# Group softmax on one core: the first tile's load and store cut into pieces of 5 and 11 groups, and the last wait put into a section of its own on SyncE

## The chip, the cores and the metric

The kernel runs on one core of a Trainium2 chip. The metric is the device time of one launch in microseconds; the time before is the median of 4 runs. A profile of one further execution shows what each engine and each DMA queue did.

## The reference

```python
def setup_inputs():
    B, N, D, G = 4, 4096, 4352, 8
    return {"x": np.random.randn(B, N, D).astype(np.float32)}

def reference(x):
    B, N, D = x.shape
    G = 8
    Dg = D // G
    x_g = x.reshape(B, N, G, Dg)
    x_g = x_g - x_g.max(axis=-1, keepdims=True)
    exp = np.exp(x_g)
    out = exp / exp.sum(axis=-1, keepdims=True)
    return out.reshape(B, N, D).astype(np.float32)
```

Each of the 16,384 rows of 4352 numbers is cut into 8 groups of 544, and a softmax is taken over each group. The input and the output are 285.2 MB each.

## The kernel before

**Tiles.** A tile holds 256 rows: 128 partitions with 2 rows each, so 8704 numbers (34,816 bytes) or 16 groups in a partition, 4.456 MB in all. There are 64 tiles (`nt`) and six buffers in SBUF (`xt0` to `xt5`, `NT = 6`); tile t lives in buffer t modulo 6 from its load to its store, and is worked on in place.

**One tile's way.** SyncE (SP) issues its load (L126). ScalarE (ACT) takes the exponential of the whole tile in one instruction (L73). VectorE (DVE) sums each group (L83), takes the reciprocals (L85) and multiplies (L88). Then the tile is stored: GpSimd (POOL) issues the stores of tiles 0 to 61 (L138), SP those of the last two tiles, 62 and 63 (L134). No maximum is subtracted on this way. VectorE keeps the largest sums and reciprocals (L96), tests them after the last tile (`judge`, L101 to L119, with a small matmul on PE), and three engines read the verdict into registers (L167); only where a number was out of bounds would all be done again with the maximum (L168 to L202). With this input that does not happen: the branch skips it.

**Order.** The order is written out by hand with semaphores, and each engine's instructions run in the order of the program. `landed[b]` counts loads into buffer b, `stored[b]` GpSimd's stores from it, `exp_done` ACT's tiles, `scaled` VectorE's, `last_stored` the two stores that SP issues; a DMA adds 16 when it has landed. SP issues loads 0 to 5 at once; before each load t from 6 on it waits until the store of tile t - 6 has landed (L123). The last tile, 63, is loaded as two DMAs of one row of each partition (L129), and ACT and VectorE work on it in two halves (`parts`). After the loads SP waits for tile 62, stores it, waits for tile 63 and stores it.

GpSimd waits for `scaled` and issues, tile by tile. After store 61 it waits until stores 58 to 61 have landed (L140), drains (L141), and waits for both of SP's last stores (L142).

**The section.** All of this stands in one critical section (L49), in which nothing is scheduled or synchronised but by the program's own semaphores. Its `sync_engine` is GpSimd: GpSimd opens the section for all engines, and at its end all engines wait until GpSimd has come to the end of its own instructions. Behind the section the program ends with barriers over all engines (L228).

**Queues.** All DMAs run on the core's same 16 DMA engines, each DMA with 8 of its 128 partitions on each of them. What SP issues is in queue 1 (the loads and the last two stores), what GpSimd issues is in queue 0.

Of the kernel before, what the change touches and what calls it, by code (L numbers as in the profile page):

```python
# [9 lines left out]
def kernel(  # L10
# [5 lines left out]
    nc = tc.nc  # L16
    G = 8
    P = 128
    R = 2
    NT = 6  # L20
# [3 lines left out]
    N, D = xf.shape  # L24
    Dg = D // G
    nt = N // (P * R)
    LAST = 2
    TURNS = 6
    LOW, HIGH = 1e-6, 1e30
    f32 = mybir.dt.float32  # L30
    X = mybir.AxisListType.X
# [2 lines left out]
    xt = xf.rearrange("(t p r) d -> t p (r d)", p=P, r=R)  # L34
    ot = of.rearrange("(t p r) d -> t p (r d)", p=P, r=R)

    landed = [tc.alloc_semaphore(f"landed{b}") for b in range(NT)]
    stored = [tc.alloc_semaphore(f"stored{b}") for b in range(NT)]
    last_landed = tc.alloc_semaphore("last_landed")
    last_stored = tc.alloc_semaphore("last_stored")  # L40
    exp_done = tc.alloc_semaphore("exp_done")
    own = tc.alloc_semaphore("own")
    scaled = tc.alloc_semaphore("scaled")
# [2 lines left out]
    judged = tc.alloc_semaphore("judged")  # L46
    again = {k: tc.alloc_semaphore(f"again_{k}") for k in ("in", "max", "exp", "rec", "out", "end")}

    ctx.enter_context(tc.tile_critical(  # L49
        sync_engine=mybir.EngineType.Pool, no_gpsimd_drain=True))  # L50
    bufs = [ctx.enter_context(nc.sbuf_tensor(f"xt{b}", [P, R * D], f32)) for b in range(NT)]
    vals = ctx.enter_context(nc.sbuf_tensor("vals", [P, NT, 2, RG], f32))
# [12 lines left out]
    def grouped(b):  # L65
        return bufs[b][:, :].rearrange("p (g d) -> p g d", d=Dg)

    def groups(t, g):
        return grouped(t % NT)[:, g, :]

    def scalar_exp(n):
        t, g = parts[n]
        i = nc.scalar.activation(out=groups(t, g), in_=groups(t, g), func=Exp, scale=1.0)  # L73
        if g.start == 0:
            i.wait_op(landed[t % NT], 16 * (t // NT + 1), "sem-ge")
        else:
            i.wait_op(last_landed, 16, "sem-ge")
        i.then_inc(exp_done, 1)

    def vector_scale(n, exp_at, at):  # L80
        t, g = parts[n]
        b = t % NT
        nc.vector.reduce_sum(out=vals[:, b, 0, g], in_=groups(t, g), axis=X).wait_op(  # L83
            exp_done, exp_at, "sem-ge").then_inc(own, 1)
        nc.vector.reciprocal(out=vals[:, b, 1, g], in_=vals[:, b, 0, g]).wait_op(  # L85
            own, at + 1, "sem-ge").then_inc(own, 1)
        xg = groups(t, g)
        nc.vector.tensor_tensor(  # L88
            out=xg,
            in0=xg,  # L90
            in1=vals[:, b, 1, g].unsqueeze(2).to_broadcast([P, g.stop - g.start, Dg]),
            op=op.mult,
        ).wait_op(own, at + 2, "sem-ge").then_inc(scaled, 1)
# [7 lines left out]
    def judge(at):  # L101
# [16 lines left out]
        nc.vector.wait_ge(tested, 5)  # L118
        nc.vector.tensor_copy(out=verdict[:, :], in_=count[:, :]).then_inc(judged, 1)  # L119

    for t in range(nt):
        if t >= NT:
            nc.sync.wait_ge(stored[t % NT], 16 * (t // NT))  # L123
        tile_in = bufs[t % NT]
        if t < nt - 1:
            nc.sync.dma_start(out=tile_in[:, :], in_=xt[t]).then_inc(landed[t % NT], 16)  # L126
        else:
            for r in range(R):
                nc.sync.dma_start(  # L129
                    out=tile_in[:, r * D:(r + 1) * D], in_=xt[t, :, r * D:(r + 1) * D],  # L130
                ).then_inc(landed[t % NT] if r < R - 1 else last_landed, 16)
# [1 line left out]
        nc.sync.wait_ge(scaled, t + 1 if t < nt - 1 else len(parts))  # L133
        nc.sync.dma_start(out=ot[t], in_=bufs[t % NT][:, :]).then_inc(last_stored, 16)  # L134

    for t in range(nt - LAST):
        nc.gpsimd.wait_ge(scaled, t + 1)
        nc.gpsimd.dma_start(out=ot[t], in_=bufs[t % NT][:, :]).then_inc(stored[t % NT], 16)  # L138
    for t in range(nt - NT, nt - LAST):
        nc.gpsimd.wait_ge(stored[t % NT], 16 * (t // NT + 1))  # L140
    nc.gpsimd.drain()  # L141
    nc.gpsimd.wait_ge(last_stored, 16 * LAST)  # L142

    nc.scalar.preload_act_table(Exp)  # L144
    for n in range(len(parts)):
        scalar_exp(n)

    nc.vector.memset(peak[:, :, :, :], 0.0).then_inc(own, 1)  # L148
    with nc.vector.Fori(0, TURNS):  # L149
        for n in range(NT):  # L150
# [4 lines left out]
    done = 1  # L155
    for n in range(TURNS * NT, len(parts)):
        vector_scale(n, n + 1 - TURNS * NT, done)
        done += 2
# [9 lines left out]
    with nc.If_cmp(regs, 2 * P, "IS_LT"):  # L168
# [3 lines left out]
        with nc.Fori(0, nt, engines=[ET.SP, ET.Activation, ET.DVE]) as t:  # L172
# [11 lines left out]
            for g in range(RG):  # L184
                i = nc.scalar.activation(
                    out=grouped(0)[:, g, :], in_=grouped(0)[:, g, :], func=Exp,
# [6 lines left out]
                out=mx[:, :], in_=grouped(0), axis=X, negate=True).then_inc(again["max"], 1)  # L193
# [6 lines left out]
                out=grouped(0), in0=grouped(0),  # L200
                in1=vals[:, 0, 1, :].unsqueeze(2).to_broadcast([P, RG, Dg]),
                op=op.mult).then_inc(again["out"], 1)  # L202


# [1 line left out]
_INS = ['x']  # L206
# [26 lines left out]
```

## Time and profile before

The median of 4 runs is 1324.55 us (1324.49 to 1325.65). The profiled execution took 1324.64 us; its span, from the first to the last instruction, is 1322.9 us, so 1.7 us lie outside the span.

| | us | of the span |
|---|---|---|
| VectorE busy (213 instructions) | 1199.7 | 91% |
| ScalarE busy (66) | 478.7 | 36% |
| GpSimd busy (66) | 33.3 | 3% |
| TensorE busy (2) | 0.2 | 0% |

Each engine's busy share in 40 equal slices of the span, in tenths, and what the DMA engines moved in each slice:

```profile
DVE  3999999999998998989989889898898988989894
ACT  4443342432424424234243342433424334243231
DMA  9999999999999999999999999999999999999999
GB/s 404 421 436 424 437 438 434 425 438 436 432 430 438 436 425 436 438 434 425 438 436 432 430 438 436 425 437 437 434 426 437 436 433 430 437 435 426 437 437 389
```

The two queues' shares of the 16 engines' span add up to 99.9%, and 570.47 MB were moved at a mean of 431 GB/s:

```profile
DMA packets 18580, 570.47 MB, mean 431 GB/s; under 512 B 2064, under 2 KB 2064, under 8 KB 2064
...
q1 hardware_dynamic: 9648, 294.13, 51.6%
q0 software_dynamic: 8928, 276.30, 48.3%
```

The costliest groups of instructions (times called, then busy us and the mean ns of one, then idle us of the engine before them and what ended it):

```profile
L73 ACT ACTIVATE xt<-xt 128x8704 f32<-128x8704 f32 (+1 forms) x65 | 477.4, 7345 | 814.7 <-DMA xt<-in_x_dram 814.7
L83 DVE TENSOR_REDUCE vals<-xt 128x16 f32<-128x8704 f32 (+1 forms) x65 | 590.1, 9078 | 100.9 <-ACT xt L73 100.0
L88 DVE TENSOR_TENSOR xt<-xt,vals 128x8704 f32<-128x8704 f32 (+1 forms) x65 | 590.5, 9085 | 2.2
L138 POOL DMA_DIRECT2D out_dram<-xt x62 | 33.1, 534 | 1232.6 <-DVE xt L88 1232.6
```

The times from issue to landing hold the waiting in the queue: 40.9 us for a load and 55.9 us for one of GpSimd's stores (medians). In the waits of SP's queue, 57 waits of a load for the store of its buffer make up 1195.5 us.

### The profile page before, as it was taken

What the parts mean: (1) busy time and instruction counts of PE and PEld (TensorE: products, weight loads), DVE (VectorE), ACT (ScalarE), POOL (GpSimd) and SP (SyncE); (2) the same over time, 40 slices, a digit from 0 to 9 for tenths busy, and PEclk for the clock granted to TensorE, in tenths of its full rate; (3) what the DMA queues carried; (4) which work ended last, traced back from release to release, by engine and by line L of the source; (5) the groups of instructions that cost most, each with busy time, mean ns of one, the idle gap of its engine ahead of it and who ended that gap; (6) DMA issues with size and microseconds to landing.
All of it is one profiled execution on the core that took longest, in us unless ns stands there. A gap on an engine that the chain in (4) does not pass through costs nothing.

```text
span 1322.9 us, 513 instructions
## 1 busy us (share of the span) xinstructions
PE 0.2 (0%) x2; PEld 0.1 (0%) x2; DVE 1199.7 (91%) x213; ACT 478.7 (36%) x66; POOL 33.3 (3%) x66
## 2 busy tenths in 40 slices
PE   0000000000000000000000000000000000000000
PEld 0000000000000000000000000000000000000000
DVE  3999999999998998989989889898898988989894
ACT  4443342432424424234243342433424334243231
POOL 0000000000000000000000000000000000000000
DMA  9999999999999999999999999999999999999999
GB/s 404 421 436 424 437 438 434 425 438 436 432 430 438 436 425 436 438 434 425 438 436 432 430 438 436 425 437 437 434 426 437 436 433 430 437 435 426 437 437 389
DMA packets 18580, 570.47 MB, mean 431 GB/s; under 512 B 2064, under 2 KB 2064, under 8 KB 2064
## 3 DMA queue, kind: packets, MB, share of 16 engines
q1 hardware_dynamic: 9648, 294.13, 51.6%
q0 software_dynamic: 8928, 276.30, 48.3%
q14 instruction: 4, 0.03, 0.0%
HBM read 285.21 MB, written 285.21 MB: 431 GB/s over the span
## 4 chain that ended last, share of the span: by engine, by line
another core or an unknown queue 66%; DMA 7%; DVE 6%; SPq 1%; ACT 1%; issue 0%; PE 0%; DVEq 0%
DMA out_dram<-xt 4%; DMA xt<-in_x_dram 3%; DVE xt L88 3%; DVE vals L83 3%; SPq L126 1%; ACT xt L73 1%; DVE vals L85 0%; DVE extreme L103 0%; DVE peak L96 0%; DVE within L109 0%; PE found L113 0%; DVE count L117 0%; DVE verdict L119 0%; DVEq L149 0%
## 5 line engine op out<-in xcount | busy, mean ns | idle before, releaser
L73 ACT ACTIVATE xt<-xt 128x8704 f32<-128x8704 f32 (+1 forms) x65 | 477.4, 7345 | 814.7 <-DMA xt<-in_x_dram 814.7
L83 DVE TENSOR_REDUCE vals<-xt 128x16 f32<-128x8704 f32 (+1 forms) x65 | 590.1, 9078 | 100.9 <-ACT xt L73 100.0
L88 DVE TENSOR_TENSOR xt<-xt,vals 128x8704 f32<-128x8704 f32 (+1 forms) x65 | 590.5, 9085 | 2.2
L138 POOL DMA_DIRECT2D out_dram<-xt x62 | 33.1, 534 | 1232.6 <-DVE xt L88 1232.6
L85 DVE RECIPROCAL vals<-vals 128x16 f32<-128x16 f32 (+1 forms) x65 | 16.3, 251 | 2.2
L96 DVE TENSOR_TENSOR peak<-peak,vals 128x192 f32<-128x192 f32 x11 | 3.9, 352 | 0.0
L144 ACT ACT_TABLE_LOAD x1 | 1.3, 1283 | 0.9 <-PEq L217 0.9
L148 DVE MEMSET peak<- 128x192 f32 x1 | 0.2, 218 | 1.1 <-PEq L217 1.1
L117 DVE TENSOR_REDUCE count<-found 1x1 f32<-1x2 f32 x1 | 0.1, 147 | 0.3 <-PE found L113 0.3
L103 DVE TENSOR_REDUCE extreme<-peak 128x2 f32<-128x192 f32 x1 | 0.3, 348 | 0.0
L113 PE MATMUL found<-within,one 128*1 128x2 f32 x2 | 0.2, 166 | 1306.0 <-DVE within L109 1306.0
L109 DVE TENSOR_SCALAR within<-extreme 128x1 f32<-128x1 f32 x2 | 0.2, 148 | 0.0
L119 DVE CAST verdict<-count 1x1 int32<-1x1 f32 x1 | 0.1, 143 | 0.0
L113 PEld LDWEIGHTS found<-within,one 128*1 128x1 f32 x2 | 0.1, 82 | 1306.0 <-DVE within L109 1306.0
L217 POOL MEMSET const-float32-0.0<- 128x1 f32 x1 | 0.1, 98 | 0.3 <-issue 0.3
L217 POOL MEMSET const-bfloat16-1.0<- 128x1 bf16 x1 | 0.1, 101 | 0.0
L217 POOL MEMSET const-uint8-127<- 128x1 uint8 x1 | 0.1, 99 | 0.0
L217 POOL MEMSET const-float32-1.0<- 128x1 f32 x1 | 0.1, 98 | 0.0
L102 DVE MEMSET one<- 128x1 f32 x1 | 0.1, 59 | 0.0
## 6 DMA issues: line engine op xcount, KB each, us to landing
xt<-in_x_dram SPq DMA_DIRECT2D x63, 4352.0 KB, 40.9
out_dram<-xt POOLq DMA_DIRECT2D x62, 4352.0 KB, 55.9
out_dram<-xt SPq DMA_DIRECT2D x2, 4352.0 KB, 20.8
xt<-in_x_dram SPq DMA_DIRECT2D x2, 2176.0 KB, 43.4
```

The lines of the kernel that those rows point to most:

```text
L73: i = nc.scalar.activation(out=groups(t, g), in_=groups(t, g), func=Exp, scale=1.0)
L83: nc.vector.reduce_sum(out=vals[:, b, 0, g], in_=groups(t, g), axis=X).wait_op(exp_done, exp_at, "sem-ge").then_inc(own, 1)
L85: nc.vector.reciprocal(out=vals[:, b, 1, g], in_=vals[:, b, 0, g]).wait_op(own, at + 1, "sem-ge").then_inc(own, 1)
L88: nc.vector.tensor_tensor(out=xg, in0=xg, in1=vals[:, b, 1, g].unsqueeze(2).to_broadcast([P, g.stop - g.start, Dg]), op=op.mult,).wait_op( ...
L96: nc.vector.tensor_tensor(out=peak[:, :, :, :], in0=peak[:, :, :, :], in1=vals[:, :, :, :], op=op.max,).wait_op(own, at, "sem-ge").then_in ...
L103: nc.vector.tensor_reduce(out=extreme[:, :], in_=peak[:, :, :, :].rearrange("p b k g -> p k b g"), axis=mybir.AxisListType.XY, op=op.max,) ...
L109: nc.vector.tensor_scalar(out=within[:, k:k + 1], in0=extreme[:, k:k + 1], scalar1=most, scalar2=None, op0=op.is_le).then_inc(tested, 1)
L113: nc.tensor.matmul(out=found[:, :], lhsT=one[:, :], rhs=within[:, :], start=True, stop=True).then_inc(counted, 1)
L126: nc.sync.dma_start(out=tile_in[:, :], in_=xt[t]).then_inc(landed[t % NT], 16)
L138: nc.gpsimd.dma_start(out=ot[t], in_=bufs[t % NT][:, :]).then_inc(stored[t % NT], 16)
L144: nc.scalar.preload_act_table(Exp)
L217: nc = _bacc.Bacc("TRN2", target_bir_lowering=False, num_devices=1)
```

## The change

The load of tile 0 is issued as two DMAs, of groups 0 to 4 and of groups 5 to 15 of each partition (10,880 and 23,936 bytes), each with its semaphore (`first_landed` and `landed[0]`). ACT waits for both before its one exponential of tile 0. The store of tile 0 is cut at the same place, on GpSimd, with `first_stored` and `stored[0]`; SP waits for both before load 6, which takes the same buffer. All other tiles are loaded, computed and stored as they were.

The critical section is closed by hand after the last line of the kernel. GpSimd's part of it ends with the drain. A second critical section, with SP as its `sync_engine`, follows; the wait for SP's last two stores stands there alone.

```diff
+    FIRST = 5
...
+    first_landed = tc.alloc_semaphore("first_landed")
+    first_stored = tc.alloc_semaphore("first_stored")
...
-    ctx.enter_context(tc.tile_critical(
+    section = ctx.enter_context(ExitStack())
+    section.enter_context(tc.tile_critical(
         sync_engine=mybir.EngineType.Pool, no_gpsimd_drain=True))
...
         t, g = parts[n]
+        if n == 0:
+            nc.scalar.wait_ge(first_landed, 16)
...
+    cut = FIRST * Dg
+    pieces = [slice(0, cut), slice(cut, R * D)]
     for t in range(nt):
+        if t == NT:
+            nc.sync.wait_ge(first_stored, 16)
         if t >= NT:
             nc.sync.wait_ge(stored[t % NT], 16 * (t // NT))
         tile_in = bufs[t % NT]
-        if t < nt - 1:
+        if t == 0:
+            for s, done in zip(pieces, (first_landed, landed[0])):
+                nc.sync.dma_start(out=tile_in[:, s], in_=xt[0, :, s]).then_inc(done, 16)
+        elif t < nt - 1:
...
-    for t in range(nt - LAST):
+    nc.gpsimd.wait_ge(scaled, 1)
+    for s, done in zip(pieces, (first_stored, stored[0])):
+        nc.gpsimd.dma_start(out=ot[0, :, s], in_=bufs[0][:, s]).then_inc(done, 16)
+    for t in range(1, nt - LAST):
         nc.gpsimd.wait_ge(scaled, t + 1)
         nc.gpsimd.dma_start(out=ot[t], in_=bufs[t % NT][:, :]).then_inc(stored[t % NT], 16)
     for t in range(nt - NT, nt - LAST):
         nc.gpsimd.wait_ge(stored[t % NT], 16 * (t // NT + 1))
     nc.gpsimd.drain()
-    nc.gpsimd.wait_ge(last_stored, 16 * LAST)
...
+    section.close()
+    with tc.tile_critical(sync_engine=mybir.EngineType.SP, no_gpsimd_drain=True):
+        nc.sync.wait_ge(last_stored, 16 * LAST)
```

## The prediction

> **What bounds the kernel now.** I read the page's busy slices first, then the table by stretches, then the timeline round the places the change touches, and last the rows of GpSimd's final instructions. The stretches come first (length; busy time and count of PE, PEld, DVE, ACT, POOL; clock; DMA share; GB/s):
>
> ```profile
> 300.00:1250.00 950.00, 0.00 (x0) 0.00 (x0) 868.74 (x148) 343.07 (x47) 24.98 (x47) 1.00 1.00 433
> 1311.30:1321.00 9.70, 0.00 (x0) 0.00 (x0) 0.00 (x0) 0.00 (x0) 0.00 (x0) 1.00 0.86 371
> 1321.00:1323.00 2.00, 0.00 (x0) 0.00 (x0) 0.00 (x0) 0.00 (x0) 0.00 (x0) 1.00 0.00 0
> ```
>
> The 16 DMA engines are full (share 1.00) from the first packets to 1321; VectorE, at 91%, always has slack. A load plus a store takes 20.56 us (20.23 + 0.33 per step in the chain of waits), and a transfer is 8 large packets on each engine (128 rows over 16), so a packet is 20.56 / 16 = 1.285 us. All 1024 packets of an engine are 1316 of the 1322.9 us; only some 7 us are outside them, so a gain over 0.2% (2.65 us, about what a measurement of this kernel can tell from no change) has little room.
>
> Next, the order of packets. The timeline (start, length, line, releaser), where stores begin:
>
> ```profile
> 34.58 7.46 ACT L73 ACTIVATE xt<-xt 128x8704 f32<-128x8704 f32 x1 [2.86 <-DMA xt<-in_x_dram]
> 40.51 0.67 POOL L138 DMA_DIRECT2D out_dram<-xt  x1 [40.06 <-DVE xt L88]
> 45.37 7.46 ACT L73 ACTIVATE xt<-xt 128x8704 f32<-128x8704 f32 x1 [3.34 <-DMA xt<-in_x_dram]
> 66.37 7.46 ACT L73 ACTIVATE xt<-xt 128x8704 f32<-128x8704 f32 x1 [13.54 <-DMA xt<-in_x_dram]
> 66.53 0.33 SPq L126 DMA_DIRECT2D xt<-in_x_dram  x1
> ```
>
> ACT's start is a load's landing: tile 3 at 45.37, tile 4 at 66.37. SP's issue at 66.53 (tile 6) is the landing of store 0. So store 0 began as load 3 ended, alternated with load 4, and both ended within 0.2 us; each later store also lands beside the load four tiles ahead (86.93 and 87.10). That the engines alternate by packets, not by bytes, is seen where tile 63 is loaded in halves, in the DMA view from 1270 to 1290:
>
> ```profile
> q0 software_dynamic: 194, 5.68, 65.7%
> q1 hardware_dynamic: 200, 3.15, 36.7%
> ```
>
> Queue 0 is GpSimd's stores, queue 1 SP's: as many packets of each, though SP's are half as large, so SP's queue gets half the bytes. Last, GpSimd's final instructions (count, min/median/max ns, first and last start):
>
> ```profile
> L140 POOLq EVENT_SEMAPHORE  x2: 17/30/43, 1290.7 to 1311.3; - x2
> L141 POOLq DRAIN  x1: 5129/5129/5129, 1311.4 to 1311.4; - x1
> L126 POOLq COMPARE_BRANCH  x1: 33/33/33, 1321.4 to 1321.4; - x1
> ```
>
> Store 61 lands at 1311.3, the drain then takes 5.13 us to 1316.5, and store 63 lands at 1321.45 (this row carries L126 but is the wait of L142). The drain is free today only because 8 packets of store 63 (8 x 1.285 = 10.3 us) run alone on SP's queue after store 61. From that wait to the end are 1322.88 - 1321.45 = 1.43 us.
>
> **Part by part.** *Split load.* ACT waits for both pieces before one unchanged ACTIVATE, so no compute begins earlier. It adds one issue on SP (0.33 to 0.55 us), covered because loads 1 to 5 are queued long before they are needed (load 5's issue ends near 4 us and becomes 4.5; its data moves after 66), and one more small packet per engine. Without that cover 0.45 us would be paid. ACT's extra wait, under 0.1 us, delays ACT alone, which has 2.86 us idle before tile 1.
>
> *Split store.* One more issue on GpSimd (0.53 us; only the next store wait is behind it, 18 us later), one more transfer in queue 0, and one more wait on SP ahead of load 6, met before the wait on the second piece. More packets cost little: in 15.45 us (ACT's starts at 1259.62 and 1275.07) 8 halves and 8 wholes pass, 12 whole-packet times of 1.285 are 15.42, so 8 extra packets cost 0.03 us; two split transfers, with the small packets, 0.06, and I allow 0.13.
>
> The Trainium skill ("DMA: Bandwidth & Descriptors", "Anatomy of one DMA — SWDGE (gpsimd) path") speaks against it: about 2.0 us fixed per DMA. Two more DMAs would cost 4 us by that and the time would be 1328.6. The 950 us row has some 92 transfers end to end at share 1.00, so here the fixed part of a queued transfer is hidden and I do not add it.
>
> The dear part is an order that shifts. Tile 0's store is now 16 packets per engine, alternating with 16 load packets: piece one with load 4, 8 x 1.285 x (5/16 + 1) = 13.5 us, piece two with load 5, 8 x 1.285 x (11/16 + 1) = 17.3 us. Store 0 thus lands near 66.5 - 20.6 + 30.8 = 76.8, together with load 5. Load 6 waits for it, so SP's queue is **empty** when store 0 ends; it was never empty before. No bandwidth is lost at once, because store 1 (issued at 59.19) fills the engines alone. Let k be the store packets that run before load 6 enters. Afterwards loads stay 8 - k packets ahead of stores, to the end: SP's queue has only k packets of store 63 left when store 61 is done, instead of 8.
>
> k is not in the trace; I bound it. From below: landing to issue 0.33 us, about 0.5 us from the last packet to the landing (an estimate: 1321.0, where the DMA rows stop, to 1321.45), and issue to first bytes 1.0 us (load 0 was issued at 0.90, the DMA records begin at 1.92) to 2.2 (it landed at 13.95; less 10.31 for the transfer, as between ACT's 24.26 and 34.58, 2.7 are left for both ends, less the 0.5). In all 1.8 to 3.0 us, in which the second or the third packet is begun: k is 2 to 3. From above: store 0, issued at 40.51, began only after load 3, at 45 or later, 4.5 us; with 0.8 that is 5.3 us or k = 5. Equal phases (k = 0) or no loss of lead (k = 8) are the far ends. I take k = 3, with one packet already committed.
>
> A queue that enters beside a full one costs too: from 34.58 to 66.37 24 packets pass, 30.84 us by the rate, 31.79 measured: 0.95 us lost at the entry of the stores. The entry of load 6 is nearest to that; I take 0.95, bounds 0 and 0.95.
>
> *Wait moved to SyncE.* SP has nothing queued behind it but the end of the program; VectorE, ACT and PE wait there for SP and GpSimd. GpSimd still waits for stores 58 to 61 and drains, and its section must close before SP's opens. A second entry costs about 0.2 us (0.71 to 0.90 at the start), a second exit up to 0.3 (as 1321.60 to 1321.88): I take 0.5, bounds -0.3 (if SP's exit replaces GpSimd's) and +0.5.
>
> **Sum** (against its own execution, 1324.64 with span 1322.9): store 63 lands at 1321.45 + 0.13 + 0.95 = 1322.53. Store 61 lands 3 x 1.285 = 3.86 earlier, at 1318.7, plus 0.1 as today; 0.1 to the drain, 5.13 for it: 1324.0. Plus 1.43 and 0.5: 1325.95. That is 3.05 later, so 1327.7, or 1327.6 against the median of 1324.55, +0.23%. Each packet of k moves it by 1.285: k = 2 gives 1328.9, k = 4 1326.3.
>
> **Rivals.** (1) *Drain exposed*, k = 2 to 4, as summed: 0.63, of it 0.45 above the bound of 1327.2. (2) *Drain still hidden*, the not slower side: load 6 enters late, k of 5 or more, or the drain needs less than 5.13 us. It decides from the point where store 61 lands more than 5.2 us before store 63. Then 1324.55 + 0.13 + (0 to 0.95) + (-0.3 to 0.5): 1324.4 to 1326.1. For it speaks the slow entry of store 0; against it that SP's issue at the start of the span was quick. 0.18. (3) *Drain at the very end*, k = 0 or 1: 1327.6 + 2 or 3 x 1.285, 1330.2 to 1331.5. Against it, SP needs 1.8 us at least, more than one packet. 0.12. (4) *The split moves no phase*: the pieces are served by bytes or reach the engines as one; the tail stays, 1324.4 to 1325.2. The equal packet counts of 1270 to 1290 speak against it. 0.07.
>
> **How the numbers follow.** The time is the likeliest case's, 1327.6; its own range is 1326.3 to 1328.9. The range runs to 1324.4 for the hidden drain and to 1329.6, leaving out most of case 3. Slower is 0.45 + 0.12 = 0.57; same 0.41 (the rest of case 1, most of 2 and 4); faster 0.02.
>
> **What would show it.** Load 4 landing near 59 instead of 66.4, load 5 and store 0 together near 77, a gap of queue 1 there; each later store landing some microseconds ahead of the load five tiles on (store 1, load 6) and no longer beside the load four tiles on; GpSimd's wait on store 61 near 1319; its drain ending after store 63 lands, SP's last wait met at once. A drain that ends before 1322 or a store 61 near 1311 would make the prediction wrong, and so would a drain of another length.

## The result, and the profile after

The changed kernel takes 1326.66 us (median of 40 runs, 1325.64 to 1329.75), the kernel before 1324.51 (60 runs): a ratio of 1.0016, 95% interval 1.0012 to 1.0021. It is 2.15 us slower, clear of the scatter, and for the most part inside the 0.2% that the prediction called no change. The forecast was slower, 1327.6 us.

The profiled execution took 1325.79 us with a span of 1324.0, one of the quicker runs of the 40. What the page showed of bounds is as it was: VectorE 1199.5 us, and full DMA queues, with 32 small packets more for the two transfers added. Page, then the same stretches as before:

```profile
DMA packets 18868, 570.47 MB, mean 431 GB/s; under 512 B 2096, under 2 KB 2096, under 8 KB 2096
q1 hardware_dynamic: 9792, 294.13, 51.5%
q0 software_dynamic: 9072, 276.30, 48.3%
...
300.00:1250.00 950.00, 0.00 (x0) 0.00 (x0) 872.87 (x148) 343.01 (x46) 24.98 (x47) 1.00 1.00 433
1311.30:1321.00 9.70, 0.00 (x0) 0.00 (x0) 0.00 (x0) 0.00 (x0) 0.00 (x0) 1.00 0.83 359
1321.00:1323.00 2.00, 0.00 (x0) 0.00 (x0) 0.00 (x0) 0.00 (x0) 0.00 (x0) 1.00 0.00 0
```

The transfers run at 433 GB/s as before and still stop at about 1321, so most of the time was not lost in moving data. The timeline of the changed kernel where the first store runs:

```profile
59.72 7.46 ACT L79 ACTIVATE xt<-xt 128x8704 f32<-128x8704 f32 x1 [7.18 <-DMA xt<-in_x_dram]
76.34 0.33 SPq L139 DMA_DIRECT2D xt<-in_x_dram  x1
77.50 7.46 ACT L79 ACTIVATE xt<-xt 128x8704 f32<-128x8704 f32 x1 [10.32 <-DMA xt<-in_x_dram]
```

Load 4 lands at 59.7 instead of 66.4. Store 0 (SP's issue of load 6 is its landing) moves from 66.5 to 76.3, beside load 5 at 77.5. The DMA view of the next 3.8 us (packets, MB, share) shows the empty queue:

```profile
q0 software_dynamic: 48, 1.67, 101.7%
q1 hardware_dynamic: 4, 0.00, 0.1%
```

In 76.5 to 80.3 only stores move; SP's four packets are small ones that end load 5. Its next large packets start at 80.5 to 81.9 by the packet records, after four packets of store 1 on most engines. At the end, the rows of GpSimd's last wait and drain, and of SP's last two stores with their times to landing:

```profile
L156 POOLq EVENT_SEMAPHORE  x2: 17/30/43, 1296.1 to 1316.7; - x2
L157 POOLq DRAIN  x1: 5211/5211/5211, 1316.8 to 1316.8; - x1
L147 SPq DMA_DIRECT2D out_dram<-xt x2: 344/344/344, 1281.3 to 1300.4; - x2
DMA to landing us min/median/max: 21.4/23.2/25.1
```

Store 61 lands at 1316.7 (before: 1311.3). Store 63, issued at 1300.4, lands 21.4 us later, at 1321.8 (before: 1321.4). The drain runs from 1316.75 to 1321.96 and now ends last, if only by 0.2 us here. Behind it come 2.07 us to the end of the span (1324.03), where 1.43 us stood behind the last wait before (end 1322.88). So this profile's 1.15 us are 0.35 of a later landing, 0.2 of drain and 0.6 of a longer exit.

### The profile page after: what moved, and what is told of

The parts are those of the page before. It is cut to its first block, busy times and chain, and to the rows that moved or that the text cites. A ratio compares the mean times of both kernels' runs of the same rounds, so it can differ in the third digit from the quotient of the medians.

```text
span 1324.0 us, 523 instructions
## 1 busy us (share of the span) xinstructions
PE 0.2 (0%) x2; PEld 0.1 (0%) x2; DVE 1199.5 (91%) x213; ACT 478.7 (36%) x66; POOL 33.8 (3%) x67
## 4 chain that ended last, share of the span: by engine, by line
another core or an unknown queue 72%; DVE 9%; DMA 6%; SPq 1%; ACT 1%; issue 0%; PE 0%; DVEq 0%
DVE xt L94 4%; DVE vals L89 4%; DMA out_dram<-xt 4%; DMA xt<-in_x_dram 2%; SPq L139 1%; ACT xt L79 1%; DVE vals L91 0%; DVE extreme L109 0%; DVE peak L102 0%; DVE within L115 0%; PE found L119 0%; DVE count L123 0%; DVE verdict L125 0%; DVEq L164 0%
```

## The experiments

Twelve runs, each beside runs of the kernel before on the same chip. Each time is a median of 11 runs (40 in the first row, 4 for the store of tile 61), the ratio with its 95% interval. The first row is the profile above. "Lead" is the time by which store 61 lands ahead of store 63, from the landing events of the profile; in brackets it is rounded to packets of 1.285 us. A DMA has 16 landing events in the trace, and the last of them is its landing.

| run | us | ratio | store 61 lands | lead | span |
|---|---|---|---|---|---|
| changed kernel, first profile | 1326.66 | 1.0016 [1.0012, 1.0021] | 1316.64 | 5.13 (4) | 1324.0 |
| changed kernel again | 1326.68 | 1.0015 [1.0006, 1.0024] | 1317.40 | 3.87 (3) | 1324.8 |
| section only | 1324.56 | 1.0000 [0.9991, 1.0009] | 1310.81 | 10.64 (8) | 1322.9 |
| pieces only | 1326.20 | 1.0011 [1.0002, 1.0020] | 1317.90 | 3.87 (3) | 1324.7 |
| store split, load whole | 1327.45 | 1.0022 [1.0013, 1.0031] | 1318.13 | 3.85 (3) | 1325.5 |
| load split, store whole | 1324.41 | 0.9999 [0.9990, 1.0008] | 1311.30 | 10.09 (8) | 1322.8 |
| cut at 8 groups | 1326.84 | 1.0016 [1.0007, 1.0025] | 1318.13 | 3.87 (3) | 1325.5 |
| store of tile 30 split instead | 1327.24 | 1.0020 [1.0011, 1.0029] | 1318.03 | 3.86 (3) | 1325.4 |
| store of tile 61 split too | 1331.00 | 1.0048 [1.0033, 1.0064] | 1321.83 | 0.17 | 1329.4 |
| load 6 later | 1326.20 | 1.0013 [1.0004, 1.0022] | 1316.94 | 5.14 (4) | 1324.3 |
| drain early | 1324.90 | 1.0003 [0.9994, 1.0012] | 1317.44 | 3.90 (3) | 1322.8 |
| no drain | 1325.95 | 1.0009 [1.0000, 1.0018] | 1317.71 | 3.88 (3) | 1324.5 |
| load cut at 1 group, store whole | 1324.60 | 0.9999 [0.9990, 1.0008] | 1311.30 | 10.01 (8) | 1322.7 |

**The changed kernel again** (no edit).

> The changed kernel once more, for a second profile. The theory (the split store takes away the lead of the loads, store 61 lands late, and GpSimd's drain of 5.2 us then ends last) expects about 1326.6, and that the profile's end follows the end of the drain: with store 61 landed at T the span is T + 0.1 + 5.2 + 2.0 (2.0 as in the first profile, 1321.96 to 1324.0). With SP's queue down to 4 packets of store 63 behind store 61 the span is 1324.0, with 3 packets about 1325.2, which is where most of its runs lie. If the end does not follow the drain, the theory falls.

The second profile shows what most of its runs look like, a span of 1324.8. GpSimd's rows:

```profile
L156 POOLq EVENT_SEMAPHORE  x2: 17/30/43, 1296.6 to 1317.4; - x2
L157 POOLq DRAIN  x1: 5211/5211/5211, 1317.5 to 1317.5; - x1
```

1317.40 + 0.11 + 5.21 + 2.07 = 1324.79, the end of the span: the end follows the drain. Store 63 landed earlier than in the first profile (1321.27 against 1321.77), yet the span is 0.8 longer, so the last transfer does not set it. The lead is 3 packets instead of 4.

The order set at the start stays. SP's issue is the landing of a store (1, then 55), ACT's start that of the load five tiles on (6, then 60):

```profile
92.96 0.33 SPq L139 DMA_DIRECT2D xt<-in_x_dram  x1
100.73 7.46 ACT L79 ACTIVATE xt<-xt 128x8704 f32<-128x8704 f32 x1 [15.65 <-DMA xt<-in_x_dram]
...
1203.98 0.33 SPq L139 DMA_DIRECT2D xt<-in_x_dram  x1
1211.72 7.46 ACT L79 ACTIVATE xt<-xt 128x8704 f32<-128x8704 f32 x1 [13.11 <-DMA xt<-in_x_dram]
```

The distance is 7.8 and 7.7 us, 6 packets of the two queues in turn, so 3 of SP's. By the medians of the 16 events it is 6.0 to 6.1 packets from store 1 to store 57 in both profiles of the changed kernel, and 15.9 in the kernel before. So the lead of 4 in the first profile did not arise at load 6. It arose where store 62 enters SP's queue, issued at 1281.3 there and at 1279.1 here: by the packet records (which name no engine; packets that follow each other without a gap make 16 rows) between load 63's last packet and its first one, three whole packets of GpSimd's stores run on 15 of the 16 engines there, two on all of them here.

**Section only.**

```diff
-    nc.gpsimd.wait_ge(last_stored, 16 * LAST)
...
+    section.close()
+    with tc.tile_critical(sync_engine=mybir.EngineType.SP, no_gpsimd_drain=True):
+        nc.sync.wait_ge(last_stored, 16 * LAST)
```

> Only the second section; tile 0 is loaded and stored whole. The theory: store 61 lands near 1311.3 as before, the drain ends near 1316.5, well before store 63 at 1321.4, and the span is 1321.4 plus the 1.3 us that SyncE's path took from its last wait to the end in the changed kernel: 1322.7, so 1324.4, no different from before. Rival A (the second section costs the time by itself): 1326.6. Rival B (the pieces cost the time as transfers): 1324.5.

1324.56: nothing lost and nothing gained. The drain is as long, but early:

```profile
L142 POOLq DRAIN  x1: 5129/5129/5129, 1310.9 to 1310.9; - x1
```

Rival A falls. Where the drain is over in time, the second section costs nothing: it opens near 1316.5, and SP waits in it for store 63.

**Pieces only.**

```diff
     nc.gpsimd.drain()
+    nc.gpsimd.wait_ge(last_stored, 16 * LAST)
...
     section.close()
-    with tc.tile_critical(sync_engine=mybir.EngineType.SP, no_gpsimd_drain=True):
-        nc.sync.wait_ge(last_stored, 16 * LAST)
```

(against the changed kernel; the drain stays where it was.)

> Only the pieces of tile 0; the wait for the last two stores stays behind the drain on GpSimd, in the one section. The theory: the drain ends last as in the changed kernel, but only 1.43 us instead of 2.0 follow it: 1326.66 - 0.57 = 1326.1. Rival A (the section itself): 1324.5. Rival B (the pieces as transfers): 1326.6, with the last store landing 2 us later than before.

1326.20. The pieces hold most of the loss, so rival A falls. The rest is the second section's exit, which is on the path once the drain ends last: 1.51 us stand behind the drain in this profile, 2.07 in the two of the changed kernel. Between the medians of the times it is 0.48, which their intervals alone would not show. Store 63 landed at 1321.77, 0.35 later than before and not 2, so rival B falls.

**Store split, load whole**, and **load split, store whole** (each is the changed kernel with one of these two edits undone, and its semaphore and wait with it):

```diff
-        if t == 0:
-            for s, done in zip(pieces, (first_landed, landed[0])):
-                nc.sync.dma_start(out=tile_in[:, s], in_=xt[0, :, s]).then_inc(done, 16)
-        elif t < nt - 1:
+        if t < nt - 1:
...
-    for s, done in zip(pieces, (first_stored, stored[0])):
-        nc.gpsimd.dma_start(out=ot[0, :, s], in_=bufs[0][:, s]).then_inc(done, 16)
-    for t in range(1, nt - LAST):
+    for t in range(nt - LAST):
```

> The changed kernel with tile 0 loaded whole, its store in two pieces. The theory: the store alone takes the lead away, so store 61 lands at 1317 to 1318, 3 or 4 packets before store 63, and the drain ends last: 1326.7, plus the 0.3 us by which load 1 landed earlier where the load was split: 1327.0. Rival B (pieces as transfers, load and store alike): half of the loss, 1325.6. Rival C (the split load sets the phase): 1324.5.

> The changed kernel with tile 0 stored whole, its load in two pieces. The theory: the loads keep their lead of 8 packets, store 61 lands near 1311, the drain is hidden, and the earlier start of 0.3 us is all that is left: 1324.2. Rival B: 1325.6. Rival C: 1326.7.

1327.45 and 1324.41: the store alone does it, and the split load alone changes nothing that can be measured. The 0.45 us above what was expected of the split store lie in one late engine: 15 of store 61's 16 landing events come by 1316.80, the last at 1318.13, and the drain waits for that one. Why it is late is not explained.

**Cut at 8 groups.**

```diff
-    FIRST = 5
+    FIRST = 8
```

> The changed kernel with tile 0 cut at 8 of 16 groups instead of 5. The theory: two pieces are 16 packets wherever the cut lies, so load 5 and store 0 still end together near 77, load 6 still finds its queue empty, the landings of stores 61 and 63 lie 3 or 4 packets apart (3.9 or 5.1 us), and the time is 1326.7 within 0.5. A rival in which the sizes 5 and 11 matter expects a clear difference, of either sign.

1326.84 with a lead of 3: between these two cuts the place does not matter, that there are two pieces does.

**The store of tile 30 split instead of tile 0's** (with the second section; SP waits for both pieces ahead of load 36):

```diff
+        if t == MID:
+            nc.gpsimd.dma_start(out=ot[t, :, :cut], in_=bufs[t % NT][:, :cut]).then_inc(mid_stored, 16)
+            nc.gpsimd.dma_start(out=ot[t, :, cut:], in_=bufs[t % NT][:, cut:]).then_inc(stored[t % NT], 16)
+            continue
```

> The second section, tile 0 whole, and instead the store of tile 30 in two pieces of 5 and 11 groups. The theory: it is no matter which store is cut. Loads and stores land in pairs up to store 29; store 30's 16 packets run beside loads 34 and 35, SP's queue is empty when load 36 is issued, and from there on the lead is 3 or 4 packets: store 61 lands 3.9 or 5.1 us before store 63, the drain ends last, 1326.5 to 1327. A rival in which the loss belongs to the start (the first packets, the first store of GpSimd) expects 1324.5.

1327.24, a little above the range. It is no matter of the start: landings come in pairs up to tile 30's store, and from there on as in the changed kernel.

**The store of tile 61 split too.**

```diff
+        if t == nt - LAST - 1:
+            nc.gpsimd.dma_start(out=ot[t, :, pieces[0]], in_=bufs[t % NT][:, pieces[0]]).then_inc(late_stored, 16)
+            nc.gpsimd.dma_start(out=ot[t, :, pieces[1]], in_=bufs[t % NT][:, pieces[1]]).then_inc(stored[t % NT], 16)
+            continue
...
+    nc.gpsimd.wait_ge(late_stored, 16)
     nc.gpsimd.drain()
```

> The changed kernel with the store of tile 61 in two pieces of 5 and 11 groups as well, each with its semaphore, both waited for ahead of the drain. The theory: 16 packets of store 61 instead of 8 alternate with the 12 that SP's queue has left, so SP's queue is done first: store 63 lands near 1318.8, store 61 near 1322.2, and the whole drain stands behind it: 1322.3 + 5.2 + 2.0 = 1329.5, time 1331.3. The data are all moved at the same time as before, so a rival that sees the loss in the transfers expects 1326.8. If the drain needs only the 2.6 us behind the last landing that it needed when issued early: 1328.7.

1331.00. The last wait and the drain:

```profile
L162 POOLq EVENT_SEMAPHORE  x1: 43/43/43, 1321.9 to 1321.9; - x1
L163 POOLq DRAIN  x1: 5292/5292/5292, 1322.0 to 1322.0; - x1
```

Store 61 now lands at 1321.83, with store 63 (1322.00, 3.2 us later than expected: SP's queue was not done first), and the whole drain stands behind all transfers. This is the largest effect of all and adds no byte: 4.3 us over the changed kernel for a landing moved 4.4 to 5.2 us back.

**Load 6 later.**

```diff
             nc.sync.wait_ge(first_stored, 16)
+            nc.sync.wait_ge(scaled, 3)
```

> The changed kernel with one more wait on SyncE ahead of load 6, for VectorE's third tile, which is done at 77.5: load 6 is issued 1.5 us later than in the changed kernel (76.3). The theory expects that this makes the kernel faster: one store packet more runs before the loads are back, so loads keep 5 packets less lead lost, store 61 lands 5 instead of 3 or 4 packets before store 63, near 1315.5, the drain ends near 1320.8, hidden, and the span is that of drain_early, 1322.8 to 1323.1: 1324.7 to 1325.0. Any rival that does not rest on the order of packets expects no gain from a later load: 1326.7 or more.

Load 6 was issued at 77.41 instead of 76.3, and by the packet records five packets of store 1 ran before it on all 16 engines, where the changed kernel has four on 15 or 16 of them. From store 1 to store 57, load t + 5 lands 8.0 packets of both queues after store t (medians of the 16 events), instead of 6.0 to 6.1. So the later load does give back one packet of lead, through the whole kernel, as the theory has it. But that makes 4 and not 5: the expectation had counted from the lead of 4 at the end of the first profile, which has only 3 on the way. The drain still ends after store 63 (1322.26 against 1322.08). The median is 0.48 below the changed kernel's, but the intervals overlap: the gain is not shown by the times.

**Drain early.**

```diff
+    nc.gpsimd.drain()
     for t in range(nt - NT, nt - LAST):
         nc.gpsimd.wait_ge(stored[t % NT], 16 * (t // NT + 1))
-    nc.gpsimd.drain()
```

> The changed kernel with GpSimd's drain put ahead of its waits for stores 58 to 61, right behind the issue of store 61. The theory, if the drain is a fixed 5.2 us: it runs at 1261 to 1266 beside other work, nothing of it is left at the end, store 61 still lands near 1317, store 63 near 1321.8, and the span is 1321.8 + 1.3 = 1323.1, the time 1324.7. If the drain lasts until the stores have landed (1316.7 or later) it is no fixed cost, and the time still falls to about 1324.7 unless it outlasts the landing by 5 us, then 1326.6. Rivals A and B: 1326.6 whatever the drain does.

1324.90, not told apart from the kernel before, with the pieces, the late store 61 and the second section all in place. The slowest of these 11 runs, 1325.59, is below the quickest of the changed kernel's 40, 1325.64. So the exposed drain is the loss. But it is no fixed 5.2 us; the rows of the drain and of the wait behind it:

```profile
L155 POOLq DRAIN  x1: 60980/60980/60980, 1259.1 to 1259.1; - x1
...
L157 POOLq EVENT_SEMAPHORE  x2: 17/30/42, 1320.1 to 1320.2; - x2
```

It lasts 60.98 us, to 1320.06, 2.6 us behind the landing of store 61 (1317.44), and before store 63 lands at 1321.34. Begun behind the landing, it ends 5.3 us after it. The order of two lines halves the time by which it outlasts the landing.

**No drain.**

```diff
-    nc.gpsimd.drain()
```

> The changed kernel without GpSimd's drain; its section closes when stores 58 to 61 have landed. The theory: store 61 still lands 3 or 4 packets (3.9 to 5.1 us) before store 63, but nothing stands behind it, and the end is store 63's landing plus 1.3 us, as with the early drain: span 1322.7 to 1323.1, time 1324.3 to 1324.8. A rival in which the shifted order itself costs (transfers, section): 1326.7.

1325.95, and the expectation missed. The program's closing barrier (L246) has drains of GpSimd of its own:

```profile
L246 POOLq DRAIN  x3: 40/119/5211, 1318.4 to 1324.2; - x3
```

The first of them, at 1318.4, now takes the 5211 ns. In the other kernels the drain in the same place takes 34 ns (46 with the early drain). Whichever drain is the first after GpSimd's stores pays. Taking the line out saves only the second section, which now runs beside the drain: from the landing of store 61 to the end of the span are 6.80 us, against 7.39 in both profiles of the changed kernel. The medians differ by 0.7, with intervals that overlap.

**Load cut at 1 group, store whole**, the version to which the runs pointed, in search of one that beats both:

```diff
-    FIRST = 5
+    FIRST = 1
```

(in the kernel with the load split and the store whole.)

> The second section and the load of tile 0 cut at 1 of 16 groups, its store whole: the version that the runs so far point to, with no lead lost and the start shortened. Load 1 landed at 24.17 with tile 0 whole and at 24.00 with 5 and 11 groups; if the first packet's length is what the start loses, one group brings up to 0.3 us more: 1324.2. If not: 1324.4, as load_split.

1324.60: no gain. Load 1 landed at 24.11. No version was found that beats the kernel before by more than the scatter.

## Why the prediction was right

Its first case, the exposed drain, is what happened. The path was right in kind at each step; k came out right by two misses that cancel, and one term of the sum was too large.

- **The shifted order** was right in place and size: load 4 near 59 (59.7), store 0 near 76.8 (76.3), an empty queue behind it, four or three packets of lead instead of 8 at the very end. In the nine profiles with a cut store of tile 0 or 30 and that of tile 61 whole, the lead is near 3 or 4 whole packets (3.85 to 3.90 or 5.13 to 5.14 us). The two splits of the store alone and of another tile show that a cut store, not the start, is the cause. That the order persists is shown by the distance of the landings at each tile between.
- **k = 3** was right for most runs, in part by luck. Four packets of store 1, not three, ran before load 6 (15 engines of 16 in the first profile, all in the second), whose first packet starts 4.1 us after its issue (76.34 to 80.46) and not 1.0 to 2.2. In turn the landing events of store 61 come 1.64 us behind its last packet (median), not the 0.5 of the prediction: one packet more of SP's queue has gone by then. Behind store 63, which ends alone, they come after 0.34. So in the second profile 4 packets are left in SP's queue when store 61's last packet ends, and 3 of lead at its landing.
- **The spread.** The runs of the changed kernel lie at about 1325.7, 1326.6 and 1327.6, 0.9 to 1.0 us apart, which is less than a packet. That the lowest group has a lead of 4 and the middle one of 3 rests on one profile each. A lead of 2 was not seen; other kernels with two sections, the drain in its place and a lead of 3 took 1327.2 to 1327.3 in their profiled runs, so the highest group need not have it.
- **The drain** was 5.21 us (5.13 in the sum). That it stands behind store 61 and decides the end is shown by moves: with store 61 landing later, the kernel loses 4.3 us more; with the drain early, the loss is gone. And in the six profiles with a cut store, both sections and the drain in its place behind a whole store 61, the span ends 7.38 to 7.39 us after store 61 lands, while store 63 lands anywhere from 1321.27 to 1322.08.
- **The second section**: 0.56 us more behind the drain in the profiles (2.07 against 1.51 with the pieces only; 0.5 in the sum).
- **The size was off by 0.95 us**, and the term that was mis-sized is "a queue that enters beside a full one costs too": 0.95 us for load 6's entry, with 0.13 for the smaller packets. Store 63 was to land 1.08 us later than before; in the nine profiles with a cut store of tile 0 or 30 and that of tile 61 whole it landed at 1321.27 to 1322.08, 0.3 us later on average (their mean is 1321.7). The loss at the entry of the stores was measured in one place, its cause unknown, and was carried to another place without a row for it. At load 6's entry the packet records show no such loss: in both profiles of the changed kernel its first packet starts 1.28 us after the packet before it on all engines (1.38 on one). The later landing of store 63 is that of the slowest engine; the median of its 16 events is 1320.3 in both, 0.3 us earlier than before (1320.6). The 0.13 was not measured by itself. Taking 1.08 - 0.3 = 0.8 off the sum leaves 1326.8.
- **The chances.** The prediction put 0.57 on a loss of over 0.2% and 0.41 on no change within 0.2%. The measured 0.16% (0.12 to 0.21) lies for the most part in the second; the mechanism came true, the size on which it leant did not.
- **Its own signs.** "A drain that ends before 1322" would have made it wrong by its letter: the first profile has 1321.96. The drain ends behind store 63 there all the same, by 0.2 us, and at 1322.72 in the second profile. Store 61 landed at 1316.6 and 1317.4, not near 1319.
- **The split load** was costed as no earlier work, which holds, but load 1 lands at 23.93 to 24.13 in the eight profiles with a load cut at 5 groups, and at 24.10 to 24.24 in the four with tile 0 loaded whole: on average 0.15 us earlier, which the working did not have.
- **The hidden drain**, the rival on the other side, was the nearest miss: by the prediction it decides where the lead exceeds 5.2 us, and the first profile's 5.13 came within a tenth of it.
- **By the Trainium skill's** fixed 2.0 us per DMA ("DMA: Bandwidth & Descriptors", "Anatomy of one DMA — SWDGE (gpsimd) path") the prediction named 4 us for the two more DMAs. That section is on DMAs that GpSimd issues, so it covers the store's alone, and by it the estimate is 2 us. The runs disagree for queued transfers: with the store cut and the drain early nothing is lost that can be told (1324.90 against 1324.52). The load cut in two, which SP issues, costs nothing either (1324.41 against 1324.55).

## What to carry to other kernels

Where two queues share the DMA engines packet by packet, the number of packets sets the order of landings: a store cut in two while both queues were full shifted one queue against the other for the rest of this kernel, though no bandwidth was lost. The load cut in two while only its own queue ran shifted nothing. Before cutting, ask which landing stands ahead of a fixed tail, here GpSimd's store ahead of its drain, and how many packets of cover it has. Here the tail, a drain, ended sooner when it was started before the transfers landed than behind the wait for them.

## What the runs showed of the hardware that was not expected

GpSimd's drain is paid once, by whichever drain comes first after its stores: 5.13 to 5.29 us if it begins behind the last landing, and even without the kernel's own drain 5.21 us in the closing barrier. Begun earlier, it waits through the stores (60.98 us) and ends 2.6 us after the last of them. What it does in that time was not tried.
